# Rotary embedding on one core: the first row of batch 0 stored in two halves behind two loads, and its head read in two transfers

## The chip, the core and the metric

The kernel runs on one core of a Trainium2 chip. The time is device microseconds (us) of one execution; the kernel before takes 316.5 us, the median of three runs (316.48 to 316.59).

A core has the engines TensorE (PE, unused here), VectorE (DVE), ScalarE (ACT), GpSimd (POOL) and SyncE (SP), and 16 DMA engines that move data between the chip's memory (HBM) and the core's SBUF of 128 partitions. SyncE and ScalarE issue transfers into hardware queues (q1 and q10 in this profile), GpSimd into one software queue (q0). [...]

## The reference, cut to what matters

```python
# x: (8, 2048, 16, 64) float32; cos, sin: (2048, 32) float32
x1, x2 = x[..., :32], x[..., 32:]
cos, sin = cos[None, :, None, :], sin[None, :, None, :]
out1 = x1 * cos - x2 * sin
out2 = x1 * sin + x2 * cos
out = np.concatenate([out1, out2], axis=-1)
```

Every element of `x` is read once (67.1 MB) and every element of the output written once (67.1 MB); the tables are 0.5 MB.

## The kernel before

**Tiles.** A batch has 2048 positions. Partition p holds the 16 consecutive positions 16p to 16p + 15, the "rows" j = 0 to 15 (`J`), each of 16 heads x 64 = 1024 elements. So a batch is 128 partitions x 16384 elements: 8 MB as float32 in memory, 4 MB as float16 in SBUF. `buf` has five such places (`NBUF`), and batch b lives in place b % 5, in float16. A load (`load`, issued at L71) casts float32 to float16 on the way, a store (`store`, issued at L81) casts back; both are issued from GpSimd, and the helper `in_ring` keeps them in the order in which the code calls them. They pass through one software queue, first in, first out.

**Rotation.** `rotate` (L92, L98, L100) is three VectorE operations on a batch or on some of its rows: v = (halves of x swapped) * sin_h, x = x * cos_h, x = x + v, in place in `buf`. `sin_h` holds the sine with its first half negated, so that one product serves both halves. ScalarE makes `sin_h` and `cos_h` from the tables at L104 to L106.

**The head.** The first two rows of batch 0 (`JA` = 2) don't come with batch 0's load. SyncE asks for them in float32 at L42, behind the sine table (L41), into the tile `head`; ScalarE casts them into `buf` at L107. They are rotated by themselves with `rotate(0, 0, JA)`, before the other 14 rows of batch 0 have landed. Row 0 is then stored by itself.

**Order on GpSimd.** load 0 (14 rows), load 1, store of row 0, loads 2 and 3 in one transfer, load 4, store of batch 0's rows 1 to 15, store 1, store 2, loads 5 and 6 in one, load 7, stores 3 and 4 in one, stores 5 and 6 in one, store 7 in two parts (9 and 5 rows). The last two rows of batch 7 are cast to float32 by ScalarE (L134) into `head` and stored by SyncE (L135) behind the part of 9 rows. A store waits on GpSimd for the rotation that it stores; loads 5 to 7 wait for the stores that free their places in `buf`. What stands behind a waiting issue on GpSimd waits with it.

Of the kernel before, what the change touches and what calls it, by code (L numbers as in the profile page):

```python
# [1 line left out]

# [4 lines left out]


@with_exitstack  # L10
def kernel(
    ctx: ExitStack,
    tc: tile.TileContext,
    x: bass.AP,
    cos: bass.AP,
    sin: bass.AP,
    out: bass.AP,
):
    nc = tc.nc
    f16 = mybir.dt.float16  # L20
    f32 = mybir.dt.float32

    B, S, H, D = x.shape
    Dh = D // 2
    P = nc.NUM_PARTITIONS
    J = S // P
    NBUF = 5

    const_pool = ctx.enter_context(tc.tile_pool(name="rope_const", bufs=1))
    io_pool = ctx.enter_context(tc.tile_pool(name="rope_io", bufs=1))  # L30
    tmp_pool = ctx.enter_context(tc.tile_pool(name="rope_tmp", bufs=1))

    JA = 2
    head = const_pool.tile([P, JA, H, D], f32)
    x0 = x[0].rearrange("(p j) h d -> p j (h d)", j=J)
    sin_f = const_pool.tile([P, J, Dh], f32)
    cos_f = const_pool.tile([P, J, Dh], f32)
    cos_h = const_pool.tile([P, J, Dh], f16)
    sin_h = const_pool.tile([P, J, D], f16)
    nc.scalar.dma_start(out=cos_f, in_=cos.rearrange("(p j) d -> p j d", j=J))  # L40
    nc.sync.dma_start(out=sin_f, in_=sin.rearrange("(p j) d -> p j d", j=J))  # L41
    nc.sync.dma_start(  # L42
        out=head.rearrange("p j h d -> p (j h d)"),
        in_=x0[:, 0:JA, :].rearrange("p j f -> p (j f)"),
    )

    buf = io_pool.tile([P, NBUF, J, H, D], f16)

    ring = []

    def in_ring(dma):
        if ring:
            tc.add_manual_dep(
                dma.ins,
                ring[-1].ins.name,
                mybir.DependencyInfo(mybir.DependencyClass.NoSync, mybir.DependencyReason.DATA),
                reason="order of the ring",
            )
        ring.append(dma)
        return dma  # L60

    def load(b, n=1):
        k = b % NBUF
        if n == 1:
            j0 = JA if b == 0 else 0
            dst = buf[:, k, j0:J, :, :].rearrange("p j h d -> p (j h d)")
            src = x[b].rearrange("(p j) h d -> p j (h d)", j=J)[:, j0:J, :].rearrange("p j f -> p (j f)")
        else:
            dst = buf[:, k : k + n, :, :, :].rearrange("p b j h d -> p b (j h d)")
            src = x[b : b + n].rearrange("b (p j) h d -> p b (j h d)", j=J)  # L70
        in_ring(nc.gpsimd.dma_start(out=dst, in_=src))  # L71

    def store(b, n=1, j0=0, j1=J):
        k = b % NBUF
        if n == 1:
            src = buf[:, k, j0:j1, :, :].rearrange("p j h d -> p (j h d)")
            dst = out[b].rearrange("(p j) h d -> p j (h d)", j=J)[:, j0:j1, :].rearrange("p j f -> p (j f)")
        else:
            src = buf[:, k : k + n, :, :, :].rearrange("p b j h d -> p b (j h d)")
            dst = out[b : b + n].rearrange("b (p j) h d -> p b (j h d)", j=J)  # L80
        return in_ring(nc.gpsimd.dma_start(out=dst, in_=src))  # L81

    def rotate(b, j0=0, j1=J):
        v = tmp_pool.tile([P, J, H, D], f16)
        n = j1 - j0
        js = slice(j0, j1)
        xt = buf[:, b % NBUF, js, :, :]
        shape = [P, n, H, 2, Dh]
        sin_b = sin_h[:, js, :].rearrange("p j (e d) -> p j e d", e=2).unsqueeze(2).to_broadcast(shape)
        cos_b = cos_h[:, js, :].unsqueeze(2).to_broadcast([P, n, 2 * H, Dh])  # L90
        xe = xt.rearrange("p j h (e d) -> p j h e d", e=2)
        nc.vector.tensor_mul(  # L92
            out=v[:, js, :, :].rearrange("p j h (e d) -> p j h e d", e=2),
            in0=xe[:, :, :, ::-1, :],
            in1=sin_b,
        )
        xw = xt.rearrange("p j h (e d) -> p j (h e) d", d=Dh)
        nc.vector.tensor_mul(out=xw, in0=xw, in1=cos_b)  # L98
        xa = xt.rearrange("p j h d -> p (j h d)")
        nc.vector.tensor_add(out=xa, in0=xa, in1=v[:, js, :, :].rearrange("p j h d -> p (j h d)"))  # L100

    load(0)
    load(1)
    nc.scalar.copy(out=sin_h[:, :, Dh:D], in_=sin_f)  # L104
    nc.scalar.mul(out=sin_h[:, :, 0:Dh], in_=sin_f, mul=-1.0)  # L105
    nc.scalar.copy(out=cos_h, in_=cos_f)  # L106
    nc.scalar.copy(  # L107
        out=buf[:, 0, 0:JA, :, :].rearrange("p j h d -> p (j h d)"),
        in_=head.rearrange("p j h d -> p (j h d)"),
    )  # L110
    rotate(0, 0, JA)
    store(0, 1, 0, 1)
    load(2, 2)
    load(4)
    rotate(0, JA, J)
    store(0, 1, 1, J)
    rotate(1)
    store(1)
    rotate(2)
    store(2)  # L120
    load(5, 2)
    load(7)
    rotate(3)
    rotate(4)
    store(3, 2)
    rotate(5)
    rotate(6)
    store(5, 2)
    rotate(7)
    gate = store(7, 1, 0, 9)  # L130
    store(7, 1, 9, J - JA)
    last = buf[:, 7 % NBUF, J - JA : J, :, :].rearrange("p j h d -> p (j h d)")
    dst = out[B - 1].rearrange("(p j) h d -> p j (h d)", j=J)[:, J - JA : J, :].rearrange("p j f -> p (j f)")
    nc.scalar.copy(out=head.rearrange("p j h d -> p (j h d)"), in_=last)  # L134
    end = nc.sync.dma_start(out=dst, in_=head.rearrange("p j h d -> p (j h d)"))  # L135
    tc.add_manual_dep(
        end.ins,
        gate.ins.name,
        mybir.DependencyInfo(mybir.DependencyClass.Sync, mybir.DependencyReason.DATA),
        reason="the last rows go out behind this part",  # L140
    )


# [1 line left out]
_INS = ['x', 'cos', 'sin']  # L145
_OUTS = [((8, 2048, 16, 64), 'float32')]


# [23 lines left out]
```

## Time and profile before

| what | value |
|---|---|
| median of three runs | 316.5 us (316.48 to 316.59) |
| the profiled execution | 316.39 us |
| its span, first to last instruction | 314.6 us |
| VectorE busy | 209.1 us in 27 operations |
| ScalarE busy | 6.7 us in 6 |
| GpSimd busy | 8.6 us in 18 |
| HBM read and written | 67.63 MB and 67.11 MB, 428 GB/s over the span |
| batch 0's load (14 rows), issue to landing | 22.5 us |
| head, issue to landing | 12.0 us |
| row 0's store, issue to landing | 25.3 us |

Times in the profile's timeline are microseconds from the start of the span. A row gives start, duration, engine, line, operation, output and inputs, a count and, in brackets, how long the engine had been idle and what ended the idle time. A "q" behind an engine's name (SPq) marks an instruction of its sequencer, a transfer's issue for example. The slices cut the span in 40 equal parts; a digit is the busy share in tenths, 9 for 90% or more. A transfer is made of packets, here one for each partition and batch, and one small packet on each DMA engine that tells of its end (a semaphore packet); the trace has a record with start, duration and size of each. The size counted is that of the written side: a load writes float16, and so shows half the bytes that it reads. A window's GB/s counts a packet where it starts, so a short window between the starts of long packets shows 0 though the engines are busy.

### The profile page before, as it was taken

The page shows a single profiled execution, that of the slowest core. Times are in us where ns is not written, and L with a number is a line of the kernel's source. Part 1 is how long each engine was busy: PE and PEld are TensorE (multiplying, and loading weights), DVE is VectorE, ACT ScalarE, POOL GpSimd, SP SyncE. Part 2 cuts the span into 40 slices and gives each one's busy share as a digit, 9 for nine tenths or more (in the row PEclk, how much of TensorE's full clock was granted, in tenths as well). Part 3 has the DMA queues.
Part 4 walks back from the last instruction along what each step waited for, and adds up shares of the span by engine and source line. Part 5 has one row for each costly group of instructions (what it writes and reads, how often), then busy time and mean ns, then how long its engine had stood idle before and what let it go on. Part 6 is the DMA issues. An engine that isn't in the chain of part 4 may idle for free.

```text
span 314.6 us, 114 instructions
## 1 busy us (share of the span) xinstructions
DVE 209.1 (66%) x27; ACT 6.7 (2%) x6; POOL 8.6 (3%) x18
## 2 busy tenths in 40 slices
DVE  0039999992499999999950000899999999910000
ACT  3200000000000000000000000000000000020000
POOL 1020000000000000000010000000000000010000
DMA  7999999999999899999999999999999999999998
GB/s 240 252 242 200 200 267 200 200 267 200 200 200 325 375 500 400 400 400 533 400 200 221 246 200 200 246 221 333 400 508 425 400 400 525 408 400 400 433 425 342
DMA packets 3104, 101.71 MB, mean 323 GB/s; under 512 B 288, under 2 KB 288, under 8 KB 672
## 3 DMA queue, kind: packets, MB, share of 16 engines
q0 software_dynamic: 2528, 99.09, 98.1%
q1 hardware_dynamic: 432, 2.36, 1.9%
q10 hardware_dynamic: 144, 0.26, 0.2%
HBM read 67.63 MB, written 67.11 MB: 428 GB/s over the span
## 4 chain that ended last, share of the span: by engine, by line
DVE 65%; another core or an unknown queue 15%; DMA 7%; ACT 1%; issue 0%; DVEq 0%; ACTq 0%; PEldq 0%
DVE buf L98 22%; DVE v L92 22%; DVE buf L100 22%; DMA buf<-in_x_dram 7%; ACT head L134 1%; DVEq L92 0%; ACTq L134 0%; PEldq L167 0%
## 5 line engine op out<-in xcount | busy, mean ns | idle before, releaser
L92 DVE TENSOR_TENSOR v<-buf,sin_h 128x16384 f16<-128x16384 f16 (+2 forms) x9 | 69.7, 7744 | 66.6 <-DMA buf<-in_x_dram 51.3
L98 DVE TENSOR_TENSOR buf<-buf,cos_h 128x16384 f16<-128x16384 f16 (+2 forms) x9 | 69.7, 7744 | 0.3
L100 DVE TENSOR_TENSOR buf<-buf,v 128x16384 f16<-128x16384 f16 (+2 forms) x9 | 69.7, 7744 | 0.3
L81 POOL DMA_DIRECT2D out_dram<-buf x8 | 4.7, 584 | 219.2 <-DVE buf L100 219.2
L134 ACT CAST head<-buf 128x2048 f32<-128x2048 f16 x1 | 1.9, 1897 | 261.3 <-DVE buf L100 261.3
L71 POOL DMA_DIRECT2D buf<-in_x_dram x6 | 3.7, 628 | 49.7 <-DMA out_dram<-buf 48.9
L107 ACT CAST buf<-head 128x2048 f16<-128x2048 f32 x1 | 1.9, 1897 | 7.1 <-DMA head<-in_x_dram 7.1
L104 ACT ACT_TABLE_LOAD x1 | 1.3, 1283 | 1.2 <-PEq L156 1.2
L104 ACT CAST sin_h<-sin_f 128x512 f16<-128x512 f32 x1 | 0.6, 617 | 2.0 <-DMA sin_f<-in_sin_dram 2.0
L105 ACT ACTIVATE sin_h<-sin_f 128x512 f16<-128x512 f32 x1 | 0.6, 624 | 0.0
L106 ACT CAST cos_h<-cos_f 128x512 f16<-128x512 f32 x1 | 0.6, 601 | 0.0
L156 POOL MEMSET const-float32-0.0<- 128x1 f32 x1 | 0.1, 98 | 0.2 <-issue 0.2
L156 POOL MEMSET const-bfloat16-1.0<- 128x1 bf16 x1 | 0.1, 101 | 0.0
L156 POOL MEMSET const-uint8-127<- 128x1 uint8 x1 | 0.1, 99 | 0.0
L156 POOL MEMSET const-float32-1.0<- 128x1 f32 x1 | 0.1, 98 | 0.0
## 6 DMA issues: line engine op xcount, KB each, us to landing
buf<-in_x_dram POOLq DMA_DIRECT2D x2, 8192.0 KB, 60.3
buf<-in_x_dram POOLq DMA_DIRECT2D x3, 4096.0 KB, 57.4
out_dram<-buf POOLq DMA_DIRECT2D x1, 7680.0 KB, 73.5
out_dram<-buf POOLq DMA_DIRECT2D x1, 4608.0 KB, 28.6
buf<-in_x_dram POOLq DMA_DIRECT2D x1, 3584.0 KB, 22.5
out_dram<-buf POOLq DMA_DIRECT2D x1, 2560.0 KB, 34.1
head<-in_x_dram SPq DMA_DIRECT2D x1, 1024.0 KB, 12.0
out_dram<-head SPq DMA_DIRECT2D x1, 1024.0 KB, 8.4
```

The source lines that it names most:

```text
L71: in_ring(nc.gpsimd.dma_start(out=dst, in_=src))
L81: return in_ring(nc.gpsimd.dma_start(out=dst, in_=src))
L92: nc.vector.tensor_mul(out=v[:, js, :, :].rearrange("p j h (e d) -> p j h e d", e=2), in0=xe[:, :, :, ::-1, :], in1=sin_b,)
L98: nc.vector.tensor_mul(out=xw, in0=xw, in1=cos_b)
L100: nc.vector.tensor_add(out=xa, in0=xa, in1=v[:, js, :, :].rearrange("p j h d -> p (j h d)"))
L104: nc.scalar.copy(out=sin_h[:, :, Dh:D], in_=sin_f)
L105: nc.scalar.mul(out=sin_h[:, :, 0:Dh], in_=sin_f, mul=-1.0)
L106: nc.scalar.copy(out=cos_h, in_=cos_f)
L107: nc.scalar.copy(out=buf[:, 0, 0:JA, :, :].rearrange("p j h d -> p (j h d)"), in_=head.rearrange("p j h d -> p (j h d)"),)
L134: nc.scalar.copy(out=head.rearrange("p j h d -> p (j h d)"), in_=last)
L156: nc = _bacc.Bacc("TRN2", target_bir_lowering=False, num_devices=1)
```

## The change

SyncE asks for the head in two transfers, one for each row, into the same tile. A new helper `narrow(j)` casts one row of it with ScalarE. A new helper `store_half(e)` stores heads 0 to 7 (e = 0) or 8 to 15 (e = 1) of row 0 of batch 0: 512 elements a partition, 2 KB of float32, in place of one row of 4 KB.

The order is new as well. Row 0 is cast and rotated alone. The load of batch 1 is issued behind the first half row's store instead of ahead of row 0's; the second half row's store follows it, ahead of the loads of batches 2 to 4. Row 1 is cast after that and rotated with the other 14 rows, so that the first rotation has one row instead of two, and the second 15 instead of 14. The store of rows 1 to 15 and all that follows are as before.

```diff
-    nc.sync.dma_start(
-        out=head.rearrange("p j h d -> p (j h d)"),
-        in_=x0[:, 0:JA, :].rearrange("p j f -> p (j f)"),
-    )
+    for j in range(JA):
+        nc.sync.dma_start(out=head[:, j, :, :].rearrange("p h d -> p (h d)"), in_=x0[:, j, :])
...
+    def store_half(e):
+        hs = slice(e * (H // 2), (e + 1) * (H // 2))
+        src = buf[:, 0, 0, hs, :].rearrange("p h d -> p (h d)")
+        dst = out[0].rearrange("(p j) h d -> p j h d", j=J)[:, 0, hs, :].rearrange("p h d -> p (h d)")
+        in_ring(nc.gpsimd.dma_start(out=dst, in_=src))
+
+    def narrow(j):
+        nc.scalar.copy(
+            out=buf[:, 0, j, :, :].rearrange("p h d -> p (h d)"),
+            in_=head[:, j, :, :].rearrange("p h d -> p (h d)"),
+        )
...
     load(0)
-    load(1)
     nc.scalar.copy(out=sin_h[:, :, Dh:D], in_=sin_f)
     nc.scalar.mul(out=sin_h[:, :, 0:Dh], in_=sin_f, mul=-1.0)
     nc.scalar.copy(out=cos_h, in_=cos_f)
-    nc.scalar.copy(
-        out=buf[:, 0, 0:JA, :, :].rearrange("p j h d -> p (j h d)"),
-        in_=head.rearrange("p j h d -> p (j h d)"),
-    )
-    rotate(0, 0, JA)
-    store(0, 1, 0, 1)
+    narrow(0)
+    rotate(0, 0, 1)
+    store_half(0)
+    load(1)
+    store_half(1)
     load(2, 2)
     load(4)
-    rotate(0, JA, J)
+    narrow(1)
+    rotate(0, 1, J)
     store(0, 1, 1, J)
```

## The prediction, made before the changed kernel was run

> **What bounds the kernel now.** I read the slices of the page first, then the queues, then windows over the stretches that the change touches, last the timeline.
>
> ```profile
> DVE  0039999992499999999950000899999999910000
> DMA  7999999999999899999999999999999999999998
> ...
> q0 software_dynamic: 2528, 99.09, 98.1%
> q1 hardware_dynamic: 432, 2.36, 1.9%
> ```
>
> VectorE has idle slices; the 16 DMA engines have none. q0, the software queue that GpSimd fills, holds them for 98.1% of the span, so time is only saved where that queue saves it. Does it pause between two transfers? The columns are stretch, length, busy time of DVE, ACT and POOL, clock, DMA share, GB/s (bytes of the packets that start in it).
>
> ```profile
> 82.46:101.78 19.32, 18.56 (x3) 0.00 (x0) 0.00 (x0) 1.00 1.00 215
> ...
> 119.89:139.20 19.31, 19.24 (x3) 0.00 (x0) 0.00 (x0) 1.00 1.02 434
> 139.20:158.52 19.32, 19.25 (x3) 0.00 (x0) 0.71 (x1) 1.00 1.02 434
> ```
>
> From its first packet to the first of the next transfer, batch 4's load (8 MB read as f32, 4 MB written as f16) takes 19.32 us, the stores of batches 1 and 2 19.31 and 19.32. In the trace's packet records each engine has 8 data packets per transfer, one behind the other: 8 x 2.413 = 19.30 (load), 8 x 2.409 = 19.27 (store). So going to the next transfer costs 0.02 to 0.05 us, and the queue is a sum of packets. Then the turn around row 0's store, which the change cuts in two:
>
> ```profile
> 40.02:40.38 0.36, 0.36 (x1) 0.00 (x0) 0.00 (x0) 1.00 3.60 728
> 40.38:42.56 2.18, 2.18 (x1) 0.00 (x0) 0.00 (x0) 1.00 0.00 0
> 42.56:43.83 1.27, 1.27 (x1) 0.00 (x0) 0.00 (x0) 1.00 1.18 400
> 43.83:44.16 0.33, 0.33 (x1) 0.00 (x0) 0.00 (x0) 1.00 7.60 1639
> ```
>
> The last packets of batch 1's load start in the first stretch, row 0's store fills the third, and batch 2's load starts at 43.83. By the packet records, averaged over the engines, the last load packet starts at 40.06 and by its pitch of 2.41 would give way at 42.47; the next load starts at 43.93. Row 0's store costs the queue 43.93 - 42.47 = 1.46 us: 8 packets at a pitch of 0.158 with the semaphore packets, together 1.27, and 0.19 by which the last load packet is stretched (2.63 us where the others have 2.43). At the turn from batch 4's load to batch 0's large store that packet has its usual 2.43.
>
> Last, the start: the timeline, and two windows over it.
>
> ```profile
> 1.17 0.43 SPq L42 DMA_DIRECT2D head<-in_x_dram  x1
> 1.24 1.21 POOL L71 DMA_DIRECT2D buf<-in_x_dram  x2 [0.80 <-PEq L167]
> ...
> 13.22 1.90 ACT L107 CAST buf<-head 128x2048 f16<-128x2048 f32 x1 [7.11 <-DMA head<-in_x_dram]
> ...
> 19.19 0.54 POOL L81 DMA_DIRECT2D out_dram<-buf  x1 [16.74 <-DVE buf L100]
> ...
> 23.87 7.63 DVE L92 TENSOR_TENSOR v<-buf,sin_h 128x14336 f16<-128x14336 f16 x1 [4.98 <-DMA buf<-in_x_dram]
> ```
>
> ```profile
> 3.65:5.48 1.83, 0.00 (x0) 1.02 (x2) 0.00 (x0) 1.00 1.06 443
> 5.48:5.94 0.46, 0.00 (x0) 0.46 (x2) 0.00 (x0) 1.00 4.71 1033
> ```
>
> From 3.65 to 5.48 the head moves alone; at 5.48 batch 0's load gets its first packets, 4.24 us after its issue at 1.24. From then on each head packet waits behind a load packet of 2.11 us, which is why the head lands at 13.2.
>
> **The change, part by part.**
>
> *The head in two transfers (SyncE).* The bytes stay; 8 packets per engine with a pitch of 0.306 us become 16. Half of 0.306 is 0.153, so 2.45 us stays 2.45; the added semaphore packet is 0.01. The nearest row for overhead is the 2 KB packets of sin and cos, pitch 0.080, 4 KB in two of them 0.160: 16 x 0.160 = 2.56. I take +0.02, range 0 to +0.11. SyncE issues one more transfer, 0.43 us, from 1.60; sin's took 1.0 from issue to its first packet (0.74 to 1.74), so row 1 is ready at 2.6 and its turn comes at 4.9. SyncE's next issue is at 305.34, so nothing queues behind it.
>
> *Row 0 rotated alone, before the load of batch 1 is issued.* Row 0's 8 packets: 3.65 + 8 x 0.153 = 4.88 on the first engine, 5.11 on the last (their starts lie 0.23 apart). Its landing is seen some 0.3 us after (batch 0's load: last packet ends 23.48, VectorE is released at 23.77): 5.4. ScalarE is busy with the tables until 6.11 anyway. Its cast of 1024 elements, between 617 ns (512) and 1897 (2048), is 617 + 512 x 0.833 = 1.04: done at 7.15. Three VectorE operations, from 1225 ns (2048) and 7625 (14336), that is 0.521 ns per element, take 3 x 0.69 plus 0.03 each: 9.3. The release of GpSimd took 0.29 (18.90 to 19.19): issue at 9.6. Behind this wait stand on GpSimd the load of batch 1 (10.1), the second half row (10.7), the loads of batches 2, 3 and 4 (by 12.5). If each needs 4.24 us before its first packet, the half row is ready at 13.8, and the queue needs it at 23.15, when batch 0's load ends. Cost 0, hidden by that load with 9.3 us to spare; without the cover each us late is a us lost.
>
> *Row 1 and the other 14 rows.* Row 1 has 4 packets out before 5.48 and 4 and its semaphore packet behind one load packet each: 5.48 + 5 x 2.26 = 16.8. Its cast ends near 18, before batch 0's load lands at 23.77. The next rotation has 15 rows in place of 14: 3 x (8.16 - 7.63) = +1.6 us, so batch 1 is rotated by 74.6 in place of 72.99. VectorE then waits 10.07 us for batch 2's load; 8.5 of it is left. Cost 0; the two stores come to the front of the queue only at 101.8 and 119.9.
>
> *The half rows in the queue.* Out goes one piece, 1.46. In come two, each of 8 packets of 2 KB, the semaphore packets (0.04) and perhaps a stretch. A software store of 2 KB rows isn't in the trace. Packet, below: half of the 4 KB store packet's slope, 0.075; above: no cheaper than the 4 KB packet, 0.158. I take 0.080, the pitch of the 2 KB packets of sin and cos, the nearest in size. Stretch, below: 0, as at batch 0's large store; above: double what the row had, 0.39. I take 0.19, as before a small store. So each half is 8 x 0.080 + 0.04 + 0.19 = 0.87, both 1.74, net +0.28. Low: 2 x (0.60 + 0.04) - 1.46 = -0.18. High: 2 x (1.27 + 0.39) - 1.46 = +1.86.
>
> *Sum.* +0.02 + 0.28 = +0.3 us. The profiled execution took 316.39 us, 1.8 of it outside its span of 314.6, and lies 0.11 under the median of 316.5: 316.7 there, 316.8 for a median.
>
> **Rivals.**
>
> *The queue runs dry behind batch 0's load (slower).* The mechanism is the wait that now stands ahead of batch 1's load. It decides once row 0's half is issued after 23.15 - 4.24 = 18.9, that is once row 0 lands after about 15.0. That happens if batch 0's load gets its first packet before about 4.3 us, since each packet of row 0 then waits behind one of the load's. If it came 1.0 us after the end of its own issue, as sin's did, at 2.85, all 8 and the semaphore packet are caught: landing near 22, issue near 26, first packet 27 to 30, 4 to 7 us dry: 322. Against it: that issue stands first on GpSimd in both kernels. If what counted were the end of both issues, 2.45, load 0 would start 3.03 after 1.85, at 4.88; row 0 would lose one or two packets to it and the half still go out by 12.
>
> *The turns are dearer.* A short store between loads stretches the load ahead, and two of them do it more than I take, or the 2 KB packets cost as much as 4 KB ones: 8 x 0.158 + 0.04 + 0.19 = 1.50 each, +1.5, 318.0. For it: the stretch is there before the only short store. Against: 2 KB table packets run at 0.080.
>
> *Each transfer holds its queue for start and receipt.* By rows, 1.0 (sin's first packet) and 0.3 (receipt), for one more transfer on each of two queues: +2.6, 319.1. Against it: the windows of 19.3 us leave at most 0.05 between transfers. [...]
>
> *A half row's writing hides under the next load (faster).* A load writes half of what it reads, so its write side has room; if both halves vanished, the queue would save the 1.46: 315.0. For it: nothing but that room. Against: the third window above, where the load starts only when the row's store has passed.
>
> **How the numbers follow.** Forecast (316.3 to 317.1) 0.66; dearer turns 0.14; dry queue 0.06; fixed part 0.03; hidden halves 0.11, of which 0.02 would be too little to tell. 0.2% is 0.63 us, about what a measurement of this kernel can tell from no change. Faster 0.09, same 0.66 + 0.02 = 0.68, slower 0.14 + 0.06 + 0.03 = 0.23. The range takes in the low bound (316.5 - 0.2 = 316.3, a little less for runs) and the high one (316.5 + 2.0): 316.2 to 318.5. It leaves out the dry queue, the fixed part and most of the hidden halves.
>
> **What would show it.** Right: the first half row's issue on GpSimd near 9.6; batch 0's load landing near 23.8; first packets of batch 1's load near 24.1, of batch 2's near 44.2; from there every transfer later by one shift of 0.2 to 0.4 us. Wrong: a stretch near 23 with a low DMA share, a cast of row 0 starting after 15, packets of the half rows with a pitch of 0.15, or a last packet of a load far over 2.6 us. If the whole kernel's time changes by over 0.63 us with the queue's sum as worked out here, the step that failed is that the queue never pauses.

## The result, and the profile after

The changed kernel takes 316.98 us (median of 19 runs, 316.83 to 317.51) against 316.50 (19 runs, 316.29 to 316.87): 1.0015 times the time before, 95% interval 1.0008 to 1.0022. That is 0.48 us, under the 0.63 that were set as no change, but on the slower side. The two profiled executions are further apart, 317.20 against 316.39 us, with spans of 315.4 and 314.6; the parts below are of those two.

The page after, its slices of the DMA engines, the queues and the issue of the head (KB each, us to landing):

```profile
DMA  9999999999999999999999999999999999999997
...
q0 software_dynamic: 2672, 99.09, 97.9%
q1 hardware_dynamic: 576, 2.36, 2.1%
...
head<-in_x_dram SPq DMA_DIRECT2D x2, 512.0 KB, 14.2
```

The engines are as full as before, the bytes are the same, and the packets are 288 more: 144 of the head (q1), 144 of the half rows (q0). The timeline after:

```profile
1.17 0.90 SPq L43 DMA_DIRECT2D head<-in_x_dram  x2
1.24 0.67 POOL L69 DMA_DIRECT2D buf<-in_x_dram  x1 [0.80 <-PEq L176]
...
6.41 1.04 ACT L88 CAST buf<-head 128x1024 f16<-128x1024 f32 x1 [0.53 <-DMA head<-in_x_dram]
...
9.94 0.53 POOL L85 DMA_DIRECT2D out_dram<-buf  x1 [8.03 <-DVE buf L110]
...
24.87 1.04 ACT L88 CAST buf<-head 128x1024 f16<-128x1024 f32 x1 [17.42 <-DMA head<-in_x_dram]
25.95 8.16 DVE L102 TENSOR_TENSOR v<-buf,sin_h 128x15360 f16<-128x15360 f16 x1 [16.32 <-ACT buf L88]
```

Row 0 is cast at 6.41 and its first half issued at 9.94, long before batch 0's load is through. Row 1, the second transfer, is cast only at 24.87. The windows after (columns as in the prediction):

```profile
23.93:24.99 1.06, 0.00 (x0) 0.12 (x1) 0.00 (x0) 1.00 2.64 587
...
43.25:43.89 0.64, 0.64 (x1) 0.00 (x0) 0.00 (x0) 1.00 0.95 266
43.89:44.95 1.06, 1.06 (x1) 0.00 (x0) 0.00 (x0) 1.00 2.63 582
...
304.64:305.41 0.77, 0.00 (x0) 0.00 (x0) 0.00 (x0) 1.00 1.05 426
```

and the same three starts in the kernel before:

```profile
23.03:23.49 0.46, 0.00 (x0) 0.00 (x0) 0.00 (x0) 1.00 5.32 1140
43.83:44.16 0.33, 0.33 (x1) 0.00 (x0) 0.00 (x0) 1.00 7.60 1639
304.57:304.90 0.33, 0.00 (x0) 0.00 (x0) 0.00 (x0) 1.00 2.43 993
```

The windows are cut so that each holds the first packets of one transfer on all 16 engines: batch 1's load, batch 2's load, the last part of batch 7's store. (The window from 43.25 is the half row ahead of batch 2's load.) The width of such a window is how far the first and the last engine are apart: 0.46 and then 0.33 us before, 1.06 after, and once there it stays: 1.05 still where batch 7's store begins, near 294, and 0.77 at that store's last part, the third line, where it was 0.33 before. So two readings describe a run. The *mean start* of batch 2's load over the engines, from the packet records, is 43.94 before and 44.22 after: +0.29. The *lag* of the last engine behind that mean is 0.22 before and 0.73 after: +0.51. Together 0.80, the 0.8 of the spans.

### The profile page after: what moved, and what is told of

It is laid out like the page before. It is cut to its first block, busy times and chain, and to the rows that moved or that the text cites. A ratio compares the mean times of both kernels' runs of the same rounds, so it can differ in the third digit from the quotient of the medians.

```text
span 315.4 us, 120 instructions
## 1 busy us (share of the span) xinstructions
DVE 209.1 (66%) x27; ACT 6.9 (2%) x7; POOL 9.1 (3%) x19
## 4 chain that ended last, share of the span: by engine, by line
DVE 66%; another core or an unknown queue 14%; DMA 7%; ACT 1%; issue 0%; SPq 0%; DVEq 0%; ACTq 0%
DVE v L102 22%; DVE buf L108 22%; DVE buf L110 22%; DMA head<-in_x_dram 7%; ACT head L143 1%; ACT buf L88 0%; SPq L43 0%; SPq L41 0%; DVEq L102 0%; ACTq L143 0%
## 5 line engine op out<-in xcount | busy, mean ns | idle before, releaser
L88 ACT CAST buf<-head 128x1024 f16<-128x1024 f32 x2 | 2.1, 1044 | 18.0 <-DMA head<-in_x_dram 18.0
## 6 DMA issues: line engine op xcount, KB each, us to landing
buf<-in_x_dram POOLq DMA_DIRECT2D x1, 3584.0 KB, 23.4
```

Of the source, the lines that this page charges most:

```text
L88: nc.scalar.copy(out=buf[:, 0, j, :, :].rearrange("p h d -> p (h d)"), in_=head[:, j, :, :].rearrange("p h d -> p (h d)"),)
```

## The experiments

Three theories. *Head*: the head's two transfers cost the time. *Stores*: the half rows do. *Order*: issuing batch 1's load later does. Their expectations were written before each run; in them "before" is the kernel before, timed on the same chip in the same sitting (its median was 316.55 to 316.67 there). The mean start and the lag come from the packet records, as does the *stretch*: how much longer the last packet of a load takes than the load's others, on the mean engine.

| run | us, median (range) | ratio to before, 95% | mean start of batch 2's load | lag there | mean start of batch 1's store |
|---|---|---|---|---|---|
| before | 316.50 (316.29 to 316.87) |  | 43.94 | 0.22 | 120.00 |
| changed | 316.98 (316.83 to 317.51) | 1.0008 to 1.0022 | 44.22 | 0.73 | 120.28 |
| after_again | 316.96 (316.87 to 317.22) | 1.0003 to 1.0021 | 44.27 | 0.46 | 120.33 |
| head_in_two | 317.25 (316.94 to 317.44) | 1.0011 to 1.0029 | 44.42 | 0.59 | 120.48 |
| head_joined | 316.30 (316.23 to 316.45) | 0.9981 to 0.9999 | 43.82 | 0.21 | 119.97 |
| head_joined_again | 316.33 (316.27 to 316.46) | 0.9980 to 0.9998 | 43.88 | 0.19 | 119.94 |
| halves_together | 316.68 (316.37 to 316.91) | 0.9991 to 1.0008 | 44.10 | 0.27 | 120.16 |
| head_by_partitions | 317.29 (317.07 to 317.76) | 1.0013 to 1.0030 | 44.80 | 0.23 | 120.86 |
| head_rows_0_and_2 | 317.30 (317.18 to 317.37) | 1.0014 to 1.0033 | 44.61 | 0.52 | 120.67 |
| row_behind_load0 | 317.23 (316.42 to 318.87) | 1.0003 to 1.0038 | 44.18 | 0.22 | 120.24 |
| load1_with_store | 316.62 (316.46 to 317.59) | 0.9995 to 1.0012 | 44.08 | 0.22 | 120.14 |
| no_early_store | 317.13 (317.01 to 317.38) | 1.0007 to 1.0025 | 42.63 | 0.44 | 120.64 |
| two_rows_two_turns | 316.67 (316.42 to 316.91) | 0.9994 to 1.0012 | 44.13 | 0.16 | 120.23 |
| one_half_early | 316.59 (316.37 to 316.90) | 0.9993 to 1.0010 | 43.16 | 0.18 | 119.99 |

In no_early_store and one_half_early no row, or half a row, stands ahead of batch 2's load; there the last column compares.

**after_again**: no edit.

> The changed kernel once more, nothing edited. Two readings of the packet records are compared in all runs: the mean over the 16 DMA engines of when each starts batch 2's load (43.94 us before, 44.22 after), and the lag of the last engine behind that mean (0.22 before, 0.73 after). If the lag belongs to the change (theories head, stores and order alike), it is again 0.5 to 0.9 and the mean 44.1 to 44.3; if it is chance of one execution, the lag comes out near 0.2 to 0.3 with a mean near 44.2. Time 316.9 to 317.1 either way.

The lag was 0.46, a little under the band that the expectation gave to the change, and over the 0.2 to 0.3 of chance: it belongs to the change, but its size differs from one execution to the next.

**head_in_two**, the change's first part alone:

```diff
-    nc.sync.dma_start(
-        out=head.rearrange("p j h d -> p (j h d)"),
-        in_=x0[:, 0:JA, :].rearrange("p j f -> p (j f)"),
-    )
+    for j in range(JA):
+        nc.sync.dma_start(out=head[:, j, :, :].rearrange("p h d -> p (h d)"), in_=x0[:, j, :])
```

> The kernel before with one edit: the head read in two transfers; it is still cast, rotated and stored as before. Theory head (the 4 KB packets of the two transfers stall at the start, unevenly over the engines, and more of them stand between the load's packets): mean start of batch 2's load 44.2 to 44.4, lag of the last engine 0.5 to 0.8, time 316.9 to 317.2. Theories stores and order (the loss is made by the half rows, or by the load of batch 1 issued later): mean 43.95, lag 0.2 to 0.3, time 316.5.

The first packets of batch 0's, batch 1's and batch 2's loads, windows of this run:

```profile
4.95:5.83 0.88, 0.00 (x0) 0.88 (x2) 0.00 (x0) 1.00 2.74 647
23.23:24.07 0.84, 0.00 (x0) 0.00 (x0) 0.00 (x0) 1.00 3.06 678
44.16:45.01 0.85, 0.85 (x1) 0.00 (x0) 0.00 (x0) 1.00 3.15 704
```

The engines are 0.88 us apart as soon as batch 0's load begins, before any store: the head did it. 0.61 us slower than before, more than the whole change; stores and order had expected none.

**head_joined**, the changed kernel with that part undone (the same diff, reversed).

> The changed kernel with one edit undone: the head comes in one transfer again; half rows and order stay as changed. Theory head: mean start of batch 2's load 43.7 to 43.9 (44.22 less the 0.42 that the head cost ahead of the first half row), lag 0.2 to 0.35, time 316.3 to 316.5. Theories stores and order: mean near 44.2, lag 0.7 as in the changed kernel, time 317.0. The first half row goes out later, near 17 us, still ahead of the end of batch 0's load.

Batch 1's and batch 2's loads:

```profile
23.70:24.06 0.36, 0.22 (x1) 0.00 (x0) 0.00 (x0) 1.00 7.23 1565
43.66:44.03 0.37, 0.37 (x1) 0.00 (x0) 0.00 (x0) 1.00 7.03 1522
```

The engines keep together, and the kernel is 0.34 us under the one before: the rest of the change, half rows and order, is a gain. So the two parts are +0.61 to +0.66 (head_in_two less before, changed less head_joined) and -0.34 to -0.29 (head_joined less before, changed less head_in_two). By its median this version beats both. No trace shows the 0.34, though: the profiled execution of the kernel before was a quick one, 316.39 against a median of 316.64 in that sitting, and there batch 1's store starts at 120.00, against 119.97 here. What the slower executions of the kernel before lose, and where, isn't on record.

**halves_together**: both half rows behind the load of batch 1, all else as before (the helper `store_half` is that of the change).

```diff
...
-    store(0, 1, 0, 1)
+    store_half(0)
+    store_half(1)
```

> The kernel before with one edit: row 0 is stored in two half rows, both behind the load of batch 1 where the whole row went. Theory head: the halves cost no more than the row, each about 0.66 us where the row cost 1.46, so the mean start of batch 2's load is 43.8 to 44.0, the lag 0.2 to 0.35, time 316.4 to 316.6. Theory stores (half rows let the engines drift apart or cost more): lag 0.5 to 0.7 or a mean above 44.1, time 316.9 and more. Theory order: as the kernel before, 43.94 and 0.22, 316.5.

The time, 316.68, is 0.08 over the band of theory head and the same as that of the kernel before in this sitting (316.64); the mean start, 44.10, is 0.10 over that band. The costs miss it too: the two halves together cost 1.58 us (from the start of batch 1's load to that of batch 2's, less 8 x 2.413), not 1.33, because the last packet of batch 1's load is stretched by 0.27, as by 0.19 in the kernel before. In head_joined each half costs 0.66, and no packet ahead of either is stretched (there 0.10 comes later, near 99). Halving the row isn't the gain by itself.

**head_by_partitions**: why does the head in two cost so much?

```diff
-    nc.sync.dma_start(
-        out=head.rearrange("p j h d -> p (j h d)"),
-        in_=x0[:, 0:JA, :].rearrange("p j f -> p (j f)"),
-    )
+    for p in (0, P // 2):
+        nc.sync.dma_start(
+            out=head[p : p + P // 2].rearrange("p j h d -> p (j h d)"),
+            in_=x0[p : p + P // 2, 0:JA, :].rearrange("p j f -> p (j f)"),
+        )
```

> The kernel before with one edit: the head comes in two transfers of 64 partitions each, so that its packets stay at 8 KB. It parts two readings of why two transfers cost 0.6 us (the kernel with only the head in two: mean start of batch 2's load 44.42, lag of the last engine 0.58, time 317.25). If it is the 4 KB packets (they stall one by one at the start, and 8 in place of 2 of them stand between the load's packets), this kernel is as the one before: mean 43.9 to 44.1, lag 0.2 to 0.35, time 316.5 to 316.7. If it is the second transfer itself, mean 44.3 to 44.5, lag 0.5 and more, time 317.1 to 317.3.

Neither. The lag stayed at 0.23, so a second transfer doesn't pull the engines apart. The mean start moved by 0.86 (that of batch 1's load by 1.06; the 0.19 of stretch that the kernel before has in between didn't come here). Each engine has four packets of the first transfer ahead of batch 0's load; the first took 0.31 us, as before, the other three 0.61 on the mean, on all engines alike. The second transfer's four, between load packets, took 0.32. Why those three took twice as long, no run shows. The edit brought a cost of its own, and leaves the question open.

**head_rows_0_and_2**: one transfer with 4 KB reads.

```diff
-        out=head.rearrange("p j h d -> p (j h d)"),
-        in_=x0[:, 0:JA, :].rearrange("p j f -> p (j f)"),
+        out=head.rearrange("p j h d -> p j (h d)"),
+        in_=x0[:, 0 : 2 * JA - 1 : 2, :],
```

> The kernel before with one edit: the head is one transfer, but of rows 0 and 2 of batch 0, which are not adjacent in memory, so that its reads are 4 KB long as in the changed kernel; row 1 of the output is therefore row 2's data with row 1's angles. It parts packet size from the number of transfers, which the run by partitions could not, since there the second transfer ran at half speed. Packet size: stretched head packets at the start, mean start of batch 2's load 44.2 to 44.4, lag of the last engine 0.4 to 0.7, time 317.0 to 317.3. Number of transfers: as before, 43.9 to 44.1, lag 0.2 to 0.3, time 316.6.

(In the run by partitions it was the first transfer that ran at half speed, 0.61 us for three of its four packets on each engine; the second's packets took 0.32.)

```profile
5.98:6.81 0.83, 0.00 (x0) 0.00 (x0) 0.00 (x0) 1.00 2.82 656
44.40:45.13 0.73, 0.73 (x1) 0.00 (x0) 0.00 (x0) 1.00 3.57 786
```

The first packets of batch 0's load come over 0.83 us with one transfer too, the lag is 0.52 and the time 317.30. It is the 4 KB reads. In the packet records of the four runs with 4 KB reads, 10 to 79 of the head packets that start ahead of batch 0's load last over 0.20 us, up to 0.82, where the usual time is 0.16; in the nine runs whose head is one transfer of 8 KB reads, none lasts longer than the usual 0.31. Why a 4 KB read stalls there and an 8 KB one doesn't, no run shows.

**row_behind_load0** and **load1_with_store** ask what saves the 0.3 us, place or time of issue. The first issues batch 1's load behind row 0's whole store; the second keeps the order of before, but lets that load wait for the rotation:

```diff
     load(0)
-    load(1)
...
     store(0, 1, 0, 1)
+    load(1)
```

> The kernel before with one edit: batch 1's load is issued behind row 0's store, which stays whole (4 KB packets); the head stays one transfer. It tells where the 0.3 us come from that the half rows and the order save. From the start of batch 0's load to that of batch 2's, less the packets of loads and head, row 0's store cost 1.46 before (1.27 of packets, 0.19 of a stretched last load packet). If the stretch belongs to the place behind batch 1's load, which is issued long before the store, the cost is 1.27, the mean start of batch 2's load 43.7 to 43.8, time 316.3 to 316.45, as with the head joined (43.82, 316.30). If the half rows save it, the cost stays 1.46, the mean 43.9 to 44.0, time 316.5 to 316.65.

```diff
...
-    load(1)
...
-    rotate(0, 0, JA)
+    turned = rotate(0, 0, JA)
+    late = load(1)
+    tc.add_manual_dep(
+        late.ins,
+        turned.ins.name,
+        mybir.DependencyInfo(mybir.DependencyClass.Sync, mybir.DependencyReason.DATA),
...
+    )
     store(0, 1, 0, 1)
```

> The kernel before with one edit: batch 1's load waits on GpSimd for the rotation of rows 0 and 1, and so is issued at about 19 us together with row 0's store, which stays behind it in the queue. If the stretch before a short store comes of a load that was issued much earlier than the store (time of issue), it goes: cost of the store 1.27, mean start of batch 2's load 43.7 to 43.8, time 316.3 to 316.45. If it comes of the place in the queue, it stays: cost 1.46, mean 43.9 to 44.0, time 316.5 to 316.65.

Both ideas fell. Behind batch 0's load the last load packet is stretched as well, by 0.35. The times of that kernel fall in two groups, six from 316.42 to 316.64 and six from 317.82 to 318.87, so that its median of 317.23 is the time of no execution; the profiled one is of the quick group, and what the others lose isn't on record. With the late issue the stretch stays, 0.21. Neither another place nor another time of issue takes it away.

**no_early_store**: the early store left away, batch 0 stored whole.

```diff
-    store(0, 1, 0, 1)
...
-    store(0, 1, 1, J)
+    store(0)
```

> The kernel before without the early store: all 16 rows of batch 0 are stored in one transfer. By the sum of packets it saves the 1.46 us of the early row and adds 8 packets' 4 KB to the large store, 8 x 0.151 = 1.21: the first packets of batch 1's store come 0.25 us earlier on the mean engine (120.00 before, 119.74 here; 119.97 with the head joined), lag 0.3 (0.45 of spread as at the start), time 316.3 to 316.45. A rival: the early store realigns the engines (spread 0.45 ahead of it, 0.32 behind it before), and without it the lag grows by 0.1 and the gain is 0.15: 316.45 to 316.55.

```profile
97.80:98.60 0.80, 0.80 (x1) 0.00 (x0) 0.00 (x0) 1.00 3.97 655
98.60:101.09 2.49, 2.46 (x2) 0.00 (x0) 0.00 (x0) 1.00 0.00 0
101.09:101.85 0.76, 0.76 (x1) 0.00 (x0) 0.00 (x0) 1.00 3.23 1380
```

These are the last packets of batch 4's load, a window in which none starts, and the first packets of the store. A load packet lasts 2.43; here the last ones last 3.18 on the mean engine. The turn that costs nothing in the kernel before costs 0.75 here, and the kernel is slower by about 0.5, not faster: batch 1's store starts at 120.64, 0.65 later than before, where 0.25 earlier was expected. Here the price went with the program's first store, to another place in the queue.

**two_rows_two_turns** tests that.

```diff
     load(2, 2)
+    store(0, 1, 1, JA)
     load(4)
...
-    store(0, 1, 1, J)
+    store(0, 1, JA, J)
```

> The kernel before with one edit: row 1 is stored early too, behind the loads of batches 2 and 3, ahead of batch 4's. It tells whether the stretch of the last load packet belongs to the program's first store or to every short store behind a load. First store alone: the second early row costs 1.27 (batch 4's load starts later by that; the large store is shorter by 1.21), no load packet over 2.5 us near 82, time 316.6 to 316.8. Every short store: 1.46 to 1.8 for the second row also, stretched load packets near 80, time 316.9 to 317.3.

Row 0's store behind batch 1's load and row 1's behind batch 3's:

```profile
42.60:44.01 1.41, 1.41 (x1) 0.00 (x0) 0.00 (x0) 1.00 1.07 363
...
82.62:83.88 1.26, 0.59 (x1) 0.00 (x0) 0.00 (x0) 1.00 1.19 406
```

The same 4 KB rows twice: the load packet ahead of the first is stretched by 0.23, none ahead of the second, whose cost is 1.27. In this run the first store alone pays. But a first store doesn't always pay: head_by_partitions and head_rows_0_and_2 store row 0 as the kernel before does, and the load packet ahead of it is stretched by 0.00 and 0.03 there. Being the first is not the whole cause.

**one_half_early**: only the first half row stands between loads (the lines against head_joined).

```diff
     load(1)
-    store_half(1)
...
+    store_half(1)
     store(0, 1, 1, J)
```

> The changed kernel with the head in one transfer and the second half row's store moved behind the load of batch 4, right ahead of the store of rows 1 to 15; only the first half row stands between loads. If a first store of 8 KB an engine is what keeps the stretch away from later turns, no load packet is stretched by more than 0.1 us on the mean engine, and the time is that of the head joined or 0.05 less: 316.2 to 316.35. If the second half row between loads was needed for it, the turn near 101 costs 0.2 to 0.75 more: 316.5 to 317.1.

The median of 316.59 is in the band of the second reading, at its edge. The profiled execution was one of the quick ones (316.41) and shows 0.03 of stretch ahead of the first half and 0.12 near 98.6. One half row doesn't do the whole of it; how the price is shared among the first stores stays open.

**head_joined_again**: no edit to head_joined.

> The changed kernel with the head in one transfer, once more, since it is the one version so far that came out under the kernel before (316.30 against 316.64, interval of the ratio 0.9981 to 0.9999). If the gain is real (no stretched load packet at the first turn, which in the kernel before takes 0.2 to 0.35 us and varies), it comes again: 316.2 to 316.4, ratio near 0.999, times close together, no load packet stretched near 21 us. If it was the luck of one chip's rounds: 316.5 to 316.7, and stretched packets at one of the first turns.

It came again, with times close together and no stretched load packet anywhere: 0.34 us under the kernel before, by the medians. Batch 1's store starts at 119.94, only 0.06 ahead of the quick execution of the kernel before.

## Why the prediction was right, point by point

*The queue is a sum of packets that never pauses: right* (the stores of batches 1 and 2 again take 19.31 and 19.32 us from first packet to first packet, 119.96 to 139.27 and 139.27 to 158.59), and more than was used. The mean start of batch 2's load was to be 44.2 and is 44.22; from there every transfer is later by the same 0.29, as forecast (0.2 to 0.4). But two terms were off, +0.41 for +0.02 and -0.13 for +0.28, and cancelled, and a third was not in the sum; that the time came out so near the forecast is luck.

*The head in two transfers: mis-sized.* "I take +0.02, range 0 to +0.11"; it is about 0.4 on the mean engine. Row 0's 8 packets took 1.51 us instead of 1.22, since 4 KB reads stall one by one at the start (17 of the 103 head packets that start ahead of batch 0's load last 0.21 to 0.82 us), and row 1's 8 took 0.168 each between load packets instead of 0.153. The step took its rate from half of an 8 KB packet, with the tables' 2 KB packets as the bound, and its count from the wrong moment: "Row 1 has 4 packets out before 5.48". Batch 0's load came at 5.02, as soon as row 0's packets were through, and all of row 1 stood behind load packets. The prediction had worked out 4.88 for the case that the end of both loads' issues counts; but with both issued first the load came at 4.95 in head_in_two, and with one at 5.51 in head_joined, so the number of issues isn't the reason. (In head_by_partitions too the load came in when the first of two head transfers was through, with four packets of that one ahead of it on each engine and the second's four between load packets; whether that is a rule, no run tests.) Batch 0's load landed at 24.64, not near 23.8. Row 1 was cast at 24.87, not near 17; VectorE began at 25.95, 1.3 us after that landing (23.4 after the issue at 1.24), and its wait for batch 2's load covered that.

*The lag was not in the sum at all.* The prediction averaged over the engines. The stalls fall on some engines and not on others, each engine works off its own packets to the end, and the span ends with the last one. That is 0.51 in the profiled pair, 0.24 in the second profile.

*The half rows: mis-sized the other way.* By the prediction "each half is 8 x 0.080 + 0.04 + 0.19 = 0.87"; 0.66 was measured. The packets took 0.077; the stretch of 0.19, assumed for every short store behind a load, came ahead of neither half, in four profiles (the changed kernel and head_joined, twice each). Net -0.13 in place of +0.28; the low end of the range, -0.18, was nearly it.

*Row 0's chain: right.* Issue of the first half at 9.94 (9.6 forecast), cast 1.04, VectorE 0.69 each.

*The rivals.* The queue didn't run dry: it would have needed row 0 after 15.0, and it was there at 6.41. (That rival's "1.0 us after the end of its own issue, as sin's did" is misread: by the prediction's own 0.74 to 1.74, the 1.0 runs from the start of the issue. Nothing hangs on it.) The turns weren't dearer: two half rows of 0.66 us each against the row's 1.46. No transfer held the queue for a start and a receipt (the "fixed part" of the chances): a half row passed in 0.66 us, 0.05 of it beyond its packets, where that rival took 1.3 for a transfer. No half row hid under a load: each took its 0.66.

*What decided it.* The slower half of the change outweighs the faster one: about +0.6 for the head, -0.3 for the rest; their sum is the +0.32 of the second sitting (316.96 against 316.64) and somewhat under the +0.48 of the first.

## What to carry to other kernels

Where one queue is full from start to end, work out the slowest of the 16 engines and not their mean: most of what one engine lost in the first 6 us was still there at 294 (engines 1.07 us apart at the start of batch 0's load, 1.05 there). Cutting a read from memory into shorter runs cost more than its bytes here (0.61 us in head_in_two), and neither half of a long packet's time (0.153) nor another transfer's short packets (2 x 0.080) told the rate (0.189 at the start, 0.168 between load packets). When a change has two parts, run each alone, even where the sum comes out as forecast.

## What the runs showed of the hardware that was not expected

- Reads of 4 KB a partition at the start stall unevenly (engines 0.7 to 1.07 us apart when batch 0's load starts, in four runs), reads of 8 KB don't (0.32 to 0.53 in nine). The kernels have no other such reads, so nothing is shown of later stages.
- The first store of the program can stretch the last load packet ahead of it: by 0.19 to 0.35 us ahead of a row of 4 KB or of two half rows together (six profiles), by 0.75 ahead of a whole batch (one); but by 0.00 and 0.03 in two others with the same row. A second row, stored later in the same kernel, did not (one). Ahead of half rows between separate loads it was at most 0.03, with 0.10 and 0.12 ahead of a later store in two of the five profiles. The cause isn't known. That the stretch varies from run to run, and makes the times of the kernel before and of row_behind_load0 vary, is argued from their spread against that of head_joined (0.22 us), not shown.
- The first of two transfers over 64 partitions each moved at half the rate after its first packet: 0.61 us in place of 0.31 for an 8 KB packet.
